# A list scheduler that counts the SBUF port of VectorE and GpSimd as a resource

## The chip, the core and the metric

The kernel runs on one core of a Trainium2 chip. The core's engines work side by side, each through its own queue in order: TensorE (PE; PEld is its weight load), VectorE (DVE), ScalarE (ACT), GpSimd (POOL) and SyncE (SP), which issues the DMAs. The metric is device time of one launch in microseconds (us); lower is better. Where one engine needs what another wrote, it waits on a semaphore.

## What is computed

Two transformer blocks of width 1024 on 512 tokens, in float32. The first has a state-space mixer (S5) and an attention that lets each query see the 128 keys with the highest index score; the second has retention, gated linear attention (GLA) and windowed attention with sinks, whose outputs are merged under gates, and a gated feed-forward layer.

```python
def reference(x, c, rel_bias, norm_g, w_ada, ...):
    x = first_block(x, c, rel_bias, norm_g, w_ada, ...)
    return second_block(x, norm_mix_pre_2, ...)

def first_block(x, c, ...):
    shift, scale, gate = split(silu(c) @ w_ada + b_ada)
    h = rms_norm(x, norm_g) * (1 + scale) + shift
    ssm_u, ssm_z, q, k, v, attn_z, q_idx, k_idx, w_idx = split(h @ w_in)
    y_ssm = s5_mixer(ssm_u, ...) * silu(ssm_z)
    y_attn = dsa_mixer(q, k, v, q_idx, k_idx, w_idx, ...) * silu(attn_z)
    return x + gate * (concat(y_ssm, y_attn) @ w_out)

def second_block(x, ...):
    (rq, rk, rv, rg, gq, gk, gv, gg, ga, sq, sk, sv, gate_logits) = split(rmsnorm(x) @ w_in)
    branches = stack(retention(rq, rk, rv), gla(gq, gk, gv, ga), swa_sinks(sq, sk, sv))
    x = x + rmsnorm(sum(sigmoid(gate_logits) * (branches @ w_branch)) @ w_out)
    h = rmsnorm(x)
    return x + rmsnorm((silu(h @ w_gate) * (h @ w_up)) @ w_down)
```

## The kernel before

A float32 product is computed from two parts of each operand: a rounded part (fp32r) and the rest. `wunit` loads a piece of a weight matrix into a tile `wr` by DMA, `copy` rounds it into `wh`, and `sub` subtracts, `wl = wr - wh`; both are 128 x 1024 and there are three buffers of each (NWH). Three matmuls then add up hi x hi, hi x lo and lo x hi in a PSUM tile `pm`. The activations are split in the same way (`split`). `proj_a` and `proj_b` are the two loops of the projections, by tokens and by output columns.

The order of the instructions is not that of the program text. `body` runs once and only records: each call on an engine object (`Engine.__getattr__`, line 439 issues them all later, so every row of the profile says L439) becomes an `Op` with its engine, its duration by a cost formula (`Engine.duration`), and the operations that it depends on. `Recorder.schedule` then walks through a simulated time: an engine that is free takes, out of its heap of ready operations, the one with the lowest key (program order, less boosts and less the length of the chain behind it), unless a buffer is missing. At one time the engines are asked in the order PE, DVE, ACT, POOL, SP. `issue` plays the list to the real engines, and each queue runs its part in that order; only data dependencies become waits on the chip.

Some operations may run on two engines: `copy` on ACT or DVE, `two` (an elementwise operation on two tensors) on DVE or POOL when nothing of it lies in PSUM. `Recorder.either` keeps both in `op.alts`. The engine that is asked takes it unless `better(op, e)` finds that the other one would finish sooner, counting what is ready there with a lower key, with a bonus of 300 ns for the other where DVE asks (YIELD). At most 24 operations are passed over in one look at a heap (`held`). By the cost formulas a `two` of 512 columns takes 610 on DVE and 1296 on POOL.

In the first 440 us lie the first block's modulation and projections, the index scores (`index_scores`: scalar_tensor_tensor on DVE), the search for the top 128 keys (`top_keys`: MAX8 and MATCH_REPLACE8 in turns on DVE), the S5 maps and phasors (`tap_map`, `s5_phasors`: many `two`) and the attention heads (`dsa_head`). The rest is the second block, where long runs of matmuls prevail.

Of the kernel before, what the change touches and what calls it, by code (L numbers as in the profile page):

```python
# [40 lines left out]
AVLATE = True  # L41
GATEAT = 3
YIELD = {("DVE", "ACT"): 300.0, ("DVE", "POOL"): 300.0}
WLIMIT = 400
NBOOST = 300
XRAHEAD = 100
# [39 lines left out]


class Op:
    __slots__ = ("idx", "eng", "call", "dur", "preds", "succs", "tiles", "key", "npred", "ready", "start", "end", "ahead", "alts", "table")


class Recorder:
# [50 lines left out]
    def either(self, *calls):  # L143

        self.options = []
        for c in calls:
            c()
        options, self.options = self.options, None
        self.record(*options[0])
        self.ops[-1].alts = {o[0]: (o[1], o[4]) for o in options}  # L150

    def record(self, eng, call, writes, reads, dur):
        if self.options is not None:
            self.options.append((eng, call, writes, reads, dur))
            return
        op = Op()
        op.alts = None
        op.table = self.table
        self.table = None
        op.idx = len(self.ops)  # L160
        op.eng, op.call, op.dur = eng, call, dur
        op.key = op.idx - self.boost
        op.ahead = self.ahead
        preds, tiles = set(), set()
        for ap in reads:
            name, cells = self._cells(ap)
            if name is None:
                continue
            tiles.add(name)
            cm = self.cells.setdefault(name, {})  # L170
            for c in cells:
                w = cm.get(c)
                if w is None:
                    w = cm[c] = [None, []]
                if w[0] is not None:
                    preds.add(w[0])
                w[1].append(op.idx)
        for ap in writes:
            name, cells = self._cells(ap)
            if name is None:  # L180
                continue
            tiles.add(name)
            cm = self.cells.setdefault(name, {})
            for c in cells:
                w = cm.get(c)
                if w is None:
                    w = cm[c] = [None, []]
                if w[0] is not None:
                    preds.add(w[0])
                preds.update(w[1])  # L190
                w[0], w[1] = op.idx, []
        preds.update(self.after)
        preds.discard(op.idx)
        op.preds = preds
        op.tiles = [t for t in tiles if t in self.info]
        self.ops.append(op)


    def schedule(self):
# [9 lines left out]
        for t in first:  # L209
            tag, bufs, _ = self.info[t]  # L210
# [3 lines left out]
        for tag, (bufs, ts) in tags.items():  # L214
# [6 lines left out]
            f, l = slot[tag]["first"], slot[tag]["last"]  # L221
# [58 lines left out]
        ready = {e: [] for e in engines}  # L280
# [15 lines left out]
        for op in ops:  # L296
            if op.npred == 0:
                arrive(op)
        dma_free = 0.0
        order = []  # L300
        freed = []
        now = 0.0
        front = 0
        choosy = True
        table = None

        def better(op, e):

            mine = now + op.alts[e][1]
            for f, (_, dur) in op.alts.items():  # L310
                if f != e:
                    t = max(free[f], now) + dur
                    for k, i in ready[f]:
                        if k < op.key and not done[i]:
                            t += ops[i].alts[f][1] if ops[i].alts else ops[i].dur
                    if t < mine + YIELD.get((e, f), 0.0):
                        return True
            return False

        while len(order) < n:  # L320
            if not events and choosy:
                choosy = False
                push(now, None)
            if not events:
                stuck = {e: [(ops[i].key, i) for _, i in ready[e]][:5] for e in engines}
                raise ValueError(f"no instruction can go on: {stuck}")
            now, _, what = heapq.heappop(events)
            if what is not None:
                for t in what:
                    left[t] -= 1  # L330
                    if left[t] == 0:
                        tag, bufs, _ = self.info[t]
                        if bufs:
                            s = slot[tag]
                            s["live"] -= 1
                            s["state"][s["pos"][t]] = 2
                            while s["lo"] < len(s["state"]) and s["state"][s["lo"]] == 2:
                                s["lo"] += 1
            if events and events[0][0] <= now:
                continue  # L340
            while front < n and done[front]:
                front += 1
            for e in engines:
                w = waiting[e]
                while w and w[0][0] <= now:
                    _, k, i = heapq.heappop(w)
                    heapq.heappush(ready[e], (k, i))
                while free[e] <= now and ready[e]:
                    held, got = [], None
                    while ready[e]:  # L350
                        k, i = heapq.heappop(ready[e])
                        op = ops[i]
                        if done[i]:
                            continue
                        if i > len(order) + op.ahead or (op.alts and choosy and better(op, e)):
                            held.append((k, i))
                            if len(held) >= 24:
                                break
                            continue
                        need = [t for t in op.tiles if self.info[t][1] and slot[self.info[t][0]]["state"][slot[self.info[t][0]]["pos"][t]] == 0]  # L360
                        if all(may_take(t, i, front) for t in need):
                            got = op
                            break
                        held.append((k, i))
                        if len(held) >= 24:
                            break
                    for h in held:
                        heapq.heappush(ready[e], h)
                    if got is None:
                        break  # L370
                    op = got
                    for t in need:
                        s = slot[self.info[t][0]]
                        s["live"] += 1
                        s["state"][s["pos"][t]] = 1
                    op.start = now
                    choosy = True
                    if op.alts:
                        op.eng = e
                        op.call, op.dur = op.alts[e]  # L380
                    if e == "SP":
                        free[e] = now + 450.0
                        dma_free = max(dma_free, now) + op.dur
                        op.end = max(dma_free, now + op.dur) + 2000.0
                    else:
                        load = 0.0
                        if e == "ACT" and op.table and op.table != table:
                            table, load = op.table, 1283.0
                        free[e] = now + load + op.dur
                        op.end = free[e]  # L390
                    push(free[e], None)
                    push(op.end + 150.0, tuple(op.tiles))
                    done[op.idx] = True
                    order.append(op)
                    for j in op.succs:
                        o2 = ops[j]
                        lat = self.LAT.get((op.eng, o2.eng), 197.0)
                        o2.ready = max(o2.ready, op.end + lat)
                        o2.npred -= 1
                        if o2.npred == 0:  # L400
                            arrive(o2)
# [4 lines left out]
def elems(ap):  # L406
    n = 1
    for _, c in ap.ap[1:]:
        n *= c
    return n  # L410


class Engine:
# [5 lines left out]
    def __getattr__(self, name):  # L419
        fn = getattr(self.real, name)  # L420

        def call(*args, **kw):
# [3 lines left out]
            writes = []  # L426
            reads = list(aps)
# [8 lines left out]
                self.rec.ahead = LOADAHEAD  # L436
            if self.eng == "ACT":
                self.rec.table = TABLES.get(args[2] if len(args) > 2 else kw.get("func"))
            self.rec.record(self.eng, lambda: fn(*args, **kw), writes, reads, self.duration(name, writes, reads, kw))  # L439
            if name == "memset":  # L440
                self.rec.ahead = 10 ** 9

        return call

    def duration(self, name, writes, reads, kw):
        out = writes[0]
# [1460 lines left out]
```

## Time and profile before

| | us |
|---|---|
| median of 3 runs | 1582.29 (1580.92 to 1583.3) |
| the profiled execution | 1583.61 |
| its span, first to last instruction | 1581.8 |
| PE busy, of the span | 1475.5 (93%) |
| DVE busy | 1040.0 (66%) |
| POOL busy | 377.6 (24%) |

The span is what the profile's rows are counted in, from the first instruction to the last; the profiled execution's own time has some 1.8 us around it. An engine's busy time is the time in which an instruction of it was under way, so an instruction that is under way and stands still counts as busy. The granted TensorE clock was 0.979 of full speed as a mean over the span.

### The profile page before, as it was taken

The numbers are of one execution on the slowest core, as the hardware profiler recorded it, in microseconds if no ns is written. First come the engines' busy times: TensorE is split into PE (matmuls) and PEld (weight loads), VectorE is DVE, ScalarE is ACT, GpSimd is POOL, SyncE is SP. The second block draws the span as 40 slices with busy tenths as digits, with TensorE's granted clock in tenths as the row PEclk, the third lists the DMA queues.
The fourth block names the chain that finished last, engine by engine and source line by source line (L and its number), as shares of the span: only waits on it lengthen the run. The fifth ranks groups of instructions, "written<-read, shape, count | busy, mean of one in ns | idle before, by whom it ended". The sixth has DMA issues, their size and how long they took to land.

```text
span 1581.8 us, 19335 instructions
## 1 busy us (share of the span) xinstructions
PE 1475.5 (93%) x7092; PEld 1210.0 (76%) x7092; DVE 1040.0 (66%) x2130; ACT 416.0 (26%) x905; POOL 377.6 (24%) x439
## 2 busy tenths in 40 slices
PE   6895988688999999989999999999999999999997
PEld 5674766577788887878887777778888888888886
DVE  5999995798874696696444777874478434443444
ACT  4351324344321132252011534431114111111010
POOL 2788741441200123020001221232120111110000
PEclk9997999899999999999999999999999999999999
DMA  8614232255613222213323223213343323333232
GB/s 235 203 40 156 82 79 51 67 149 180 213 49 127 62 78 83 81 35 99 106 81 120 94 67 105 69 54 106 118 151 118 106 88 99 107 96 104 81 133 107
DMA packets 169455, 165.26 MB, mean 104 GB/s; under 512 B 36992, under 2 KB 136200, under 8 KB 169232
## 3 DMA queue, kind: packets, MB, share of 16 engines
q1 hardware_dynamic: 169360, 164.02, 33.1%
q8 instruction: 56, 0.92, 0.2%
q14 instruction: 39, 0.32, 0.1%
HBM read 150.64 MB, written 10.47 MB: 102 GB/s over the span
## 4 chain that ended last, share of the span: by engine, by line
PE 65%; DVE 13%; DMA 2%; issue 2%; ACT 1%; POOL 1%; SPq 0%; DVEq 0%; ACTq 0%; POOLq 0%
PE pm L439 65%; DVE t L439 9%; DVE s L439 2%; DVE wl L439 1%; ACT t L439 1%; DMA wr<-w_in 1%; DMA wr<-w_ada 1%; POOL t L439 1%; DVE wh L439 1%; DVE c L439 0%; DMA t<-t 0%; SPq L439 0%; DMA t<-gla_w_alpha 0%; ACT L439 0%; ACT s L439 0%
## 5 line engine op out<-in xcount | busy, mean ns | idle before, releaser
L439 PE MATMUL pm<-c,wh 128*128 128x512 f32 (+1 forms) x1952 | 568.9, 388 | 4.5 <-DVE wh L439 2.5
L439 PEld LDWEIGHTS pm<-c,wh 128*128 128x128 f32 x1952 | 359.1, 189 | 75.5 <-DVE wh L439 3.4
L439 POOL TENSOR_TENSOR t<-t,t 128x512 f32<-128x512 f32 (+11 forms) x282 | 261.7, 941 | 627.7 <-ACT t L439 421.2
L439 DVE CAST wh<-wr 128x1024 fp32r<-128x1024 f32 x160 | 113.9, 712 | 356.4 <-PE pm L439 344.2
L439 PE MATMUL pm<-c,wl 128*128 128x512 f32 (+1 forms) x976 | 325.5, 387 | 0.6 <-DVE wl L439 0.5
L439 ACT ACTIVATE t<-pm 128x512 f32<-128x512 f32 (+8 forms) x315 | 150.1, 502 | 510.9 <-PE pm L439 488.0
L439 PE MATMUL pm<-t,t 128*128 128x256 f32 (+4 forms) x1232 | 242.3, 324 | 30.9 <-DVE t L439 18.2
L439 DVE TENSOR_TENSOR wl<-wr,wh 128x1024 fp32r<-128x1024 f32 (+2 forms) x195 | 244.1, 1255 | 24.3 <-PE pm L439 9.3
L439 PEld LDWEIGHTS pm<-t,t 128*128 128x128 f32 (+1 forms) x1232 | 193.7, 191 | 62.8 <-issue 14.2
L439 PEld LDWEIGHTS pm<-c,wl 128*128 128x128 f32 x976 | 183.1, 189 | 36.8 <-DVE wl L439 1.4
L439 PE MATMUL pm<-wh,c 128*128 128x512 f32 (+1 forms) x576 | 177.6, 391 | 4.0 <-DVE wh L439 2.5
L439 PE MATMUL pm<-c,t 128*128 128x128 f32 (+4 forms) x638 | 123.7, 307 | 30.9 <-DVE t L439 14.7
L439 PE MATMUL pm<-wh,t 128*128 128x512 f32 x480 | 142.2, 390 | 0.3 <-POOL t L439 0.3
L439 ACT ACTIVATE t<-t 128x512 fp32r<-128x512 f32 (+6 forms) x140 | 79.0, 581 | 229.2 <-DVE t L439 168.3
L439 PE MATMUL pm<-t,wh 128*128 128x512 f32 x416 | 137.2, 391 | 0.0
L439 PEld LDWEIGHTS pm<-c,t 128*128 128x128 f32 (+3 forms) x638 | 82.8, 152 | 64.2 <-issue 16.2
L439 PEld LDWEIGHTS pm<-wh,c 128*128 128x128 f32 x576 | 108.3, 192 | 26.9 <-DVE wh L439 3.2
L439 POOL TENSOR_TENSOR wl<-wr,wh 128x1024 fp32r<-128x1024 f32 (+1 forms) x17 | 42.7, 2513 | 320.6 <-DVE wh L439 200.6
L439 PE MATMUL pm<-wl,c 128*128 128x512 f32 (+1 forms) x288 | 104.6, 394 | 15.0 <-DVE wl L439 15.0
L439 ACT ACTIVATE wh<-wr 128x1024 fp32r<-128x1024 f32 (+2 forms) x52 | 52.9, 1019 | 203.9 <-PE pm L439 149.6
L439 PEld LDWEIGHTS pm<-wh,t 128*128 128x128 f32 x480 | 90.0, 188 | 20.0 <-POOL t L439 0.7
L439 DVE TENSOR_TENSOR t<-pm,t 64x256 f32<-64x256 f32 (+8 forms) x157 | 85.2, 557 | 24.8 <-ACT t L439 17.8
(113 smaller groups left out, 1346.4 us busy)
## 6 DMA issues: line engine op xcount, KB each, us to landing
wr<-w_in SPq DMA_DIRECT2D x48, 1024.0 KB, 5.0
wr<-w_branch SPq DMA_DIRECT2D x12, 1024.0 KB, 5.2
wr<-ffn_w_gate SPq DMA_DIRECT2D x11, 1024.0 KB, 5.2
wr<-ffn_w_up SPq DMA_DIRECT2D x11, 1024.0 KB, 5.2
wr<-ffn_w_down SPq DMA_DIRECT2D x10, 1024.0 KB, 5.0
wa<-w_ada SPq DMA_DIRECT2D x32, 256.0 KB, 4.3
wr<-w_out SPq DMA_DIRECT2D x8, 1024.0 KB, 4.9
wr<-w_in SPq DMA_DIRECT2D x12, 512.0 KB, 3.8
```

The source lines that it names most:

```text
L439: self.rec.record(self.eng, lambda: fn(*args, **kw), writes, reads, self.duration(name, writes, reads, kw))
```

## The change

Each recorded operation gets a flag `port`. `Engine.port` sets it: for POOL on all but `memset`; for DVE on operations with two or more SBUF inputs of more than one element per partition, and on `tensor_copy` and `tensor_scalar` (without `accum_out`) from SBUF to SBUF. The schedule keeps one time `port` until which the port is taken. An operation with the flag is passed over while that time lies ahead, and one that is taken sets it to its own end less HANDOVER, 60 ns on DVE and 150 ns on POOL; at that time the engines are asked again. The functions that choose between engines, the keys and the durations stay as they are, and `better` does not read the port.

```diff
--- before.py
+++ after.py
@@ -41,6 +41,7 @@
 AVLATE = True
 GATEAT = 3
 YIELD = {("DVE", "ACT"): 300.0, ("DVE", "POOL"): 300.0}
+HANDOVER = {"DVE": 60.0, "POOL": 150.0}
 WLIMIT = 400
 NBOOST = 300
 XRAHEAD = 100
@@ -86,7 +87,7 @@
 
 
 class Op:
-    __slots__ = ("idx", "eng", "call", "dur", "preds", "succs", "tiles", "key", "npred", "ready", "start", "end", "ahead", "alts", "table")
+    __slots__ = ("idx", "eng", "call", "dur", "preds", "succs", "tiles", "key", "npred", "ready", "start", "end", "ahead", "alts", "table", "port")
 
 
 class Recorder:
@@ -147,18 +148,18 @@
             c()
         options, self.options = self.options, None
         self.record(*options[0])
-        self.ops[-1].alts = {o[0]: (o[1], o[4]) for o in options}
-
-    def record(self, eng, call, writes, reads, dur):
+        self.ops[-1].alts = {o[0]: (o[1], o[4], o[5]) for o in options}
+
+    def record(self, eng, call, writes, reads, dur, port=False):
         if self.options is not None:
-            self.options.append((eng, call, writes, reads, dur))
+            self.options.append((eng, call, writes, reads, dur, port))
             return
         op = Op()
         op.alts = None
         op.table = self.table
         self.table = None
         op.idx = len(self.ops)
-        op.eng, op.call, op.dur = eng, call, dur
+        op.eng, op.call, op.dur, op.port = eng, call, dur, port
         op.key = op.idx - self.boost
         op.ahead = self.ahead
         preds, tiles = set(), set()
@@ -297,6 +298,7 @@
             if op.npred == 0:
                 arrive(op)
         dma_free = 0.0
+        port = 0.0
         order = []
         freed = []
         now = 0.0
@@ -307,7 +309,7 @@
         def better(op, e):
 
             mine = now + op.alts[e][1]
-            for f, (_, dur) in op.alts.items():
+            for f, (_, dur, _) in op.alts.items():
                 if f != e:
                     t = max(free[f], now) + dur
                     for k, i in ready[f]:
@@ -352,6 +354,11 @@
                         op = ops[i]
                         if done[i]:
                             continue
+                        if port > now and (op.alts[e][2] if op.alts else op.port):
+                            held.append((k, i))
+                            if len(held) >= 24:
+                                break
+                            continue
                         if i > len(order) + op.ahead or (op.alts and choosy and better(op, e)):
                             held.append((k, i))
                             if len(held) >= 24:
@@ -377,7 +384,10 @@
                     choosy = True
                     if op.alts:
                         op.eng = e
-                        op.call, op.dur = op.alts[e]
+                        op.call, op.dur, op.port = op.alts[e]
+                    if op.port:
+                        port = now + max(0.0, op.dur - HANDOVER[e])
+                        push(port, None)
                     if e == "SP":
                         free[e] = now + 450.0
                         dma_free = max(dma_free, now) + op.dur
@@ -436,11 +446,22 @@
                 self.rec.ahead = LOADAHEAD
             if self.eng == "ACT":
                 self.rec.table = TABLES.get(args[2] if len(args) > 2 else kw.get("func"))
-            self.rec.record(self.eng, lambda: fn(*args, **kw), writes, reads, self.duration(name, writes, reads, kw))
+            self.rec.record(self.eng, lambda: fn(*args, **kw), writes, reads, self.duration(name, writes, reads, kw),
+                            self.port(name, writes, reads, kw))
             if name == "memset":
                 self.rec.ahead = 10 ** 9
 
         return call
+
+    def port(self, name, writes, reads, kw):
+
+        if self.eng == "POOL":
+            return name != "memset"
+        if self.eng != "DVE":
+            return False
+        big = [r for r in reads if elems(r) > 1 and not self.in_psum(r)]
+        copies = name in ("tensor_copy", "tensor_scalar") and "accum_out" not in kw
+        return len(big) > 1 or (len(big) == 1 and copies and not self.in_psum(writes[0]))
 
     def duration(self, name, writes, reads, kw):
         out = writes[0]
```

## Rows read from the trace of the kernel before

**Rows 1.** the page: busy us by engine; POOL in 40 slices of 39.5 us.

```profile
PE 1475.5 (93%) x7092; PEld 1210.0 (76%) x7092; DVE 1040.0 (66%) x2130; ACT 416.0 (26%) x905; POOL 377.6 (24%) x439
...
POOL 2788741441200123020001221232120111110000
```

**Rows 2.** windows: stretch, length, busy us (xinstructions) by engine, granted clock, DMA share, GB/s.

```profile
0.00:40.00 40.00, 27.24 (x99) 20.44 (x100) 23.85 (x110) 16.02 (x35) 7.94 (x23) 0.91 0.89 234
40.00:240.00 200.00, 165.60 (x752) 128.37 (x750) 194.37 (x490) 65.96 (x136) 144.08 (x208) 0.94 0.37 111
240.00:440.00 200.00, 169.95 (x947) 141.18 (x948) 156.04 (x296) 81.62 (x189) 64.27 (x90) 0.93 0.43 131
440.00:1560.00 1120.00, 1099.18 (x5239) 909.19 (x5238) 652.71 (x1196) 249.67 (x538) 161.30 (x118) 1.00 0.29 94
1560.00:1581.80 21.80, 13.48 (x60) 10.84 (x58) 13.07 (x43) 2.75 (x8) 0.00 (x0) 0.90 0.25 96
```

**Rows 3.** waits, 240:440: us in total, times, longest.

```profile
PE pm L439 <- DVE t L439: 20.7, 11, 8.3
```

**Rows 4.** timeline, 100 to 160 us: start, us, engine, line, operation, count [idle before].

```profile
103.07 0.18 DVE L439 TENSOR_TENSOR t<-t 128x32 f32<-128x32 f32 x1
111.37 8.98 POOL L439 TENSOR_TENSOR t<-t,t 128x512 f32<-128x512 f32 x7
115.45 1.10 DVE L439 TENSOR_TENSOR t<-t 128x32 f32<-128x32 f32 x1
...
119.07 31.34 POOL L439 TENSOR_TENSOR t<-t,t 128x512 f32<-128x512 f32 x23
...
132.46 0.79 PE L439 MATMUL pm<-wl,c 128*128 128x512 f32 x1 [14.45 <-DVE wl L439]
```

**Rows 5.** groups by shape, DVE, 40:240: count, busy us, mean ns, idle before.

```profile
L439 DVE TENSOR_TENSOR wl<-wr,wh 128x1024 fp32r<-128x1024 f32 x14 | 19.8, 1417 | 0.1
L439 DVE TENSOR_TENSOR t<-t 128x32 f32<-128x32 f32 x47 | 15.5, 348 | 0.5 <-POOL t L439 0.2
L439 DVE MAX8 s<-t 128x8 f32<-128x512 f32 x16 | 10.8, 675 | 0.0
L439 DVE SCALAR_TENSOR_TENSOR t<-t,c,t 128x256 f32<-128x256 f32 x7 | 8.6, 1225 | 0.0
L439 DVE SCALAR_TENSOR_TENSOR t<-t,c,t 128x384 f32<-128x384 f32 x7 | 8.1, 1160 | 0.0
L439 DVE MATCH_REPLACE8 t<-s,t 128x512 f32<-128x512 f32 x15 | 10.0, 670 | 0.0
L439 DVE SCALAR_TENSOR_TENSOR t<-wa,c,t 128x256 f32<-128x256 f32 x16 | 7.8, 487 | 0.1
```

**Rows 6.** groups by shape, DVE, 440:520.

```profile
L439 DVE TENSOR_TENSOR wl<-wr,wh 128x1024 fp32r<-128x1024 f32 x11 | 13.3, 1222 | 2.0 <-ACT wh L439 1.8
L439 DVE TENSOR_TENSOR t<-t,t 128x512 f32<-128x512 f32 x2 | 1.4, 688 | 0.0
```

**Rows 7.** groups by shape, DVE, 240:440.

```profile
L439 DVE TENSOR_TENSOR t<-t,t 128x512 f32<-128x512 f32 x28 | 28.6, 1029 | 2.4 <-DMA t<-t 1.2 <-ACT t L439 0.8
L439 DVE TENSOR_TENSOR t<-wr,t 128x512 fp32r<-128x512 f32 x6 | 5.9, 1039 | 0.0
```

**Rows 8.** groups by shape, DVE, 440:1560.

```profile
L439 DVE TENSOR_TENSOR wl<-wr,wh 128x1024 fp32r<-128x1024 f32 x164 | 206.2, 1260 | 24.0 <-PE pm L439 9.3 <-ACT wh L439 5.7 <-issue 2.7
L439 DVE TENSOR_TENSOR t<-t,s 128x512 f32<-128x512 f32 x16 | 18.0, 1156 | 0.1
```

**Rows 9.** windows of instructions on pm alone: PE, PEld, DVE, ACT, clock, DMA.

```profile
40.00:240.00 200.00, 165.60 (x752) 128.37 (x750) 14.58 (x27) 46.64 (x107) 0.94 0.37 111
240.00:440.00 200.00, 169.95 (x947) 141.18 (x948) 52.14 (x103) 29.95 (x68) 0.93 0.43 131
```

**Rows 10.** groups by shape, POOL, 40:240.

```profile
L439 POOL TENSOR_TENSOR t<-t,t 128x512 f32<-128x512 f32 x48 | 63.6, 1348 | 0.1
```

**Rows 11.** groups by shape, POOL, 440:1560.

```profile
L439 POOL TENSOR_TENSOR wl<-wr,wh 128x1024 fp32r<-128x1024 f32 x9 | 23.9, 2651 | 207.5 <-DVE wh L439 111.7 <-PE pm L439 69.4 <-ACT wh L439 24.2
```

## The prediction

> **What bounds the kernel now.** I read the page's busy line first. TensorE (PE) is busy 1475.5 of 1581.8 us [rows 1], so PE is the bound as a whole and only its 106.3 us of idle time can come back, plus what a lowered clock costs. The windows then say where that idle time lies [rows 2]. In stretch A (40 to 240 us) PE is idle 200 - 165.60 = 34.4 us, in B (240 to 440 us) 30.0, in the long stretch C (440 to 1560 us) 1120 - 1099.18 = 20.8, at the start 12.8 and in the last 22 us 8.3. The reader is to see the DVE column beside it: VectorE (DVE) is busy 194.37 of 200 us in A, 156.04 in B, but 652.71 of 1120 in C. So A is bound by DVE, B partly, C by PE. The waits of PE agree: in B 20.7 us of them end with DVE tiles t [rows 3], and the longest of all, in A, ends with a DVE tile wl (below).
>
> Next I ask whether DVE in A works or waits. The timeline shows it [rows 4]. One and the same kind of DVE operation, 128x32 with its inputs in SBUF, takes 0.18 us at 103 us and 1.10 us at 115 us. GpSimd (POOL) runs 7 operations of 128x512 without a pause from 111.37 us on, and 23 more from 119.07 on, in 31.34 us. PE's 14.45 us wait, which ends at 132.46, falls in this time: the weight part wl that it needs stands in DVE's queue behind the stretched operations. So what counts as DVE busy holds waiting inside the instructions, and it is there only when POOL works.
>
> By shape it is as clear [rows 5]. In A the two-input SBUF operations are long: 1417 ns for a 128x1024 subtraction, 1225 ns for a scalar_tensor_tensor of 128x256. The 128x256 form whose input is a wa tile takes 487 ns. MAX8, with one input, takes 675 ns for 512 columns under the same POOL load. Where POOL does next to nothing (440 to 520 us, slices 12 and 13 of POOL's line in [rows 1]) the subtraction takes 1222 ns and a two-input 128x512 operation 688 ns [rows 6].
>
> **What the change does, part by part.** It alters only the plan that is made before the program is issued: which engine gets an operation that two could do, and the order on each engine. It adds no instruction, no DMA and no wait on the chip; the same arithmetic is issued. SP's queue is not a port user, and its DMAs move only as far as their producers or buffers move. So every gain or loss is a matter of order and of who does what.
>
> First, the wait in DVE that could be filled. In A, from [rows 5] against [rows 6] or against the shorter rows: wl 14 x (1417 - 1222) = 2.7 us; 128x32 47 x (348 - 180) = 7.9 us, with the 0.18 us of [rows 4]; 128x256 7 x (1225 - 487) = 5.2 us; 128x384 7 x (1160 - 590) = 4.0 us, where 590 is an estimate, halfway between 487 (256 columns) and 688 (512). Sum 19.8 us. In B the two largest groups [rows 7]: 28 x (1029 - 688) = 9.5 and 6 x (1039 - 688) = 2.1, sum 11.6 us. In C [rows 8]: 16 x (1156 - 688) = 7.5 and 164 x (1260 - 1222) = 6.2, sum 13.7 us.
>
> Second, how much of it returns. A wait is gained only when the planner has a DVE operation at hand that it does not count as a port user. Those are the ones with a PSUM input, 14.58 us in A and 52.14 in B [rows 9], and MAX8: 10.8 us for 512 columns [rows 5], and with the 384 and 256 widths in proportion (an estimate) 10.8 x 1152 / 512 = 24 us. That is 39 of 194 us in A, a fifth, and 52 of 156 in B, a third. Bounds of the share returned are 0 (those operations already run beside POOL, or are not ready) and 1 (every wait filled). I take a quarter in A and a third in B: A 5 us, B 4 us. In C PE is the bound and three weight buffers cover most DVE delays; PE's 20.8 us of idle time there is the ceiling. I take 2 us of 13.7; it costs up to 13.7 us if the cover fails.
>
> Third, what moves away from POOL. A 128x512 operation holds POOL 1348 ns in A, 48 times [rows 10]; DVE does it in 688 [rows 6]. With the port taken, POOL gets fewer of them and DVE more, and each that moves frees the port for 1348 - 688 = 0.66 us but costs DVE 0.69. While DVE waits behind POOL this is nearly a trade; I put 2 us gained on it, between 0 and 48 x 0.66 / 2 = 16 us (half of them moved). The casts that ScalarE may take as well are no help: the rule that picks between two engines does not look at the port, so ScalarE leaves a cast to a DVE that is free but barred. I count 0 there; ScalarE is busy only 65.96 of 200 us in A [rows 2] and would cover it.
>
> Start and tail: POOL is busy 7.94 us and 0 us there [rows 2], so 0. Sum: -5 - 4 - 2 - 2 = -13 us. The profiled execution took 1583.6 us (span 1581.8); it lies 1.3 us above the median of 1582.3. So 1583.6 - 13 = 1570.6, against the median 1569.3. I say 1570.
>
> A rule of the Trainium skill speaks against one detail. The trace shows MATCH_REPLACE8 at 670 ns for 512 columns, beside MAX8 at 675 and not stretched [rows 5]; the change marks it as a port user, since it reads the values and the eight maxima, and bars it while POOL works. "SBUF — State Buffer", section "Who interferes with whom", says that a DVE instruction with at most one SBUF input outside the two-port modes does not meet GpSimd at all; the row agrees that nothing is stretched. Were it unmarked, its 15 x 3 widths would add some 22 us of filler, and A's share would be a third: 7 us instead of 5.
>
> **Rivals.** (1) The port is full anyway. In A, DVE's 194.37 less 39 us of unmarked work is 155 us, and POOL has 144.08 [rows 2]: 299 us of port users in 200 us. If a single holder at a time is the truth, A lasts as long as its holders do, and order changes nothing; B and C lose their gain to the same. Against it: part of the 299 us is waiting, counted twice (19.8 us at least). It gives 0 in A, -2 in B, 0 else: about 1581. The Trainium skill, "SBUF — State Buffer", section "Who interferes with whom", says just this, an exclusive lock that is held for the whole instruction; by that rule A would keep its length unless operations leave POOL, about 1581 us again, and the 1.10 us of the 128x32 row agree with a lock.
>
> (2) Nothing happens because the plan is not followed. No semaphore ties the two engines to their turns, so the turns hold only as long as the plan's clock is right. The 14.45 us that PE waits in A [rows 4] are a sign that plan and chip differ. It gives 1583 plus or minus 3.
>
> (3) Slower: POOL wins the handover. In the plan the port comes free 60 ns before a DVE operation ends, while DVE itself is still taken; an idle POOL with something ready takes it then, every time, and holds it for a whole operation: 1348 ns in A [rows 10], 2651 ns for a wl in C [rows 11]. Meanwhile DVE is given less urgent work, and if that outlasts POOL's end, POOL takes the port again. Weights for PE (cast and wl, on DVE) come late. Place: A and B, and in C wherever POOL has a run. It decides when the extra turns on PE's path outnumber the gain: 13 / 1.35, some 10 turns. With 17 of them, 10 more than pay for 9 us: 1583 - 13 + 17 x 1.35 = 1593. For it: 118 POOL instructions in C, where little is to be gained. Against it: on the chip the two take turns already [rows 4], so most of these waits are in the old time too.
>
> (4) All the blocked time of A and B returns and half of what POOL gives up: 1583.6 - 31.4 - 8 = 1544.
>
> **How the numbers follow.** Forecast (1558 to 1579): 0.50. Rivals (1) and (2): 0.16 together, within 0.2% (3.2 us, about what a measurement of this kernel can tell from no change) for the most part; (3): 0.26; (4): 0.08. Faster: 0.50 + 0.08 + 0.02 from (1) = 0.60; same 0.15 (0.14 and 0.01 of the third); slower 0.25. The range leaves out half of (4) and the upper third of (3): 1549 to 1592.
>
> **What would show it.** Right: in 40 to 240 us the 128x32 and 128x256 two-input rows on DVE fall towards 180 and 487 ns, POOL has fewer 128x512 operations, and the wait of PE for wl shrinks from 14.45 us. C's PE idle time stays near 21 us. Rival (1): the stretched rows shrink, yet PE's idle time in A stays 34 us. Rival (2): those rows keep their means. Rival (3): PE's idle time in C grows, its waits ending on DVE wh and wl. The forecast is wrong if the first 440 us do not get shorter, whatever DVE's rows do.

## The result and the profile after

The changed kernel takes 1557.82 us (1556.93 to 1561.91, 4 runs) beside 1581.61 for the one before: a ratio of 0.9854, 95% interval 0.9833 to 0.9874, 23.8 us less. I had forecast 13 us less. The profiled execution took 1556.93 us, its span is 1555.1 us, 26.7 less than before.

The page of after: busy time by engine, POOL's 40 slices, and the shares of the chain that ended last.

```profile
PE 1465.6 (94%) x7092; PEld 1210.6 (78%) x7092; DVE 1000.6 (64%) x2098; ACT 434.1 (28%) x911; POOL 373.2 (24%) x465
...
POOL 1148694662200123020000232332210111110000
...
PE 74%; DVE 5%; DMA 1%; ACT 1%; issue 1%; POOL 1%; SPq 0%; DVEq 0%; ACTq 0%; POOLq 0%
```

The same chain line of before:

```profile
PE 65%; DVE 13%; DMA 2%; issue 2%; ACT 1%; POOL 1%; SPq 0%; DVEq 0%; ACTq 0%; POOLq 0%
```

PE is busy 9.9 us less than in [rows 1] and idle 1555.1 - 1465.6 = 89.5 us against 106.3. DVE is busy 39.4 us less. The reader is to see the chain: DVE's share of it fell from 13% to 5%. What the page does not show is where. The windows of after for stretches A and B are (columns as in [rows 2]):

```profile
40.00:240.00 200.00, 171.19 (x819) 138.68 (x819) 183.11 (x481) 70.63 (x124) 122.17 (x234) 0.93 0.36 110
240.00:440.00 200.00, 166.36 (x902) 135.62 (x902) 164.99 (x318) 80.70 (x193) 83.54 (x95) 0.93 0.45 133
```

In A PE is idle 28.8 us (34.4 in [rows 2]), in B 33.6 (30.0). So A and B together gained 2 us by this measure, where I had looked for 9. The stretches hold other work than before, though, so I cut both runs where the work itself cuts them. SP writes the result of the first block to the tensor scr_xd in 8 DMAs, and that of the second block's mixers in 8 more. Timeline of SP in after, merged rows that end with the 8th and with the 16th of these writes:

```profile
425.94 15.13 SPq L449 DMA_DIRECT2D scr_xd<-t  x5
...
1174.24 13.44 SPq L449 DMA_DIRECT2D scr_xd<-t  x6
```

The 8th starts at 440.7 us and the 16th at 1187.4; in before they start at 447.8 and 1214.1. Windows by these stages, the first block, the mixers, the feed-forward layer, before:

```profile
0.00:447.80 447.80, 370.10 (x1832) 295.84 (x1833) 381.40 (x912) 166.20 (x364) 216.29 (x321) 0.94 0.44 130
447.80:1214.10 766.30, 747.14 (x3609) 615.36 (x3608) 504.18 (x1008) 208.51 (x471) 129.50 (x97) 1.00 0.29 92
1214.10:1581.80 367.70, 358.22 (x1656) 298.83 (x1654) 154.46 (x212) 41.31 (x72) 31.80 (x21) 0.99 0.31 101
```

and after:

```profile
0.00:440.70 440.70, 365.55 (x1833) 295.97 (x1834) 373.80 (x904) 169.01 (x352) 210.09 (x341) 0.93 0.45 132
440.70:1187.40 746.70, 741.77 (x3608) 615.78 (x3606) 472.38 (x985) 223.84 (x489) 131.23 (x103) 1.00 0.30 94
1187.40:1555.10 367.70, 358.24 (x1656) 298.87 (x1653) 154.45 (x212) 41.30 (x72) 31.87 (x21) 0.99 0.30 101
```

Of the 26.7 us, 7.1 were gained in the first block, 19.6 in the mixers (766.3 to 746.7), and 0.0 in the feed-forward layer. PE's idle time in the mixers went from 766.30 - 747.14 = 19.2 us to 4.9. The other 5.4 us left its busy time, though the number of matmuls is the same within one. They are pauses too. In the profile a matmul of 512 columns lasts some 0.39 us where the next one starts 0.23 us after it, so the first part of each pause counts as busy. Counted by starts (each interval to the next matmul, less the median interval for its shape, where it is over 30 ns longer), pauses make up 45.0 us of the mixers before and 26.2 after, some 19 us less.

### The profile page after: what moved, and what is told of

The parts are those of the page before. It is cut to its first block, busy times and chain, and to the rows that moved or that the text cites. A ratio compares the mean times of both kernels' runs of the same rounds, so it can differ in the third digit from the quotient of the medians.

```text
span 1555.1 us, 19327 instructions
## 1 busy us (share of the span) xinstructions
PE 1465.6 (94%) x7092; PEld 1210.6 (78%) x7092; DVE 1000.6 (64%) x2098; ACT 434.1 (28%) x911; POOL 373.2 (24%) x465
## 4 chain that ended last, share of the span: by engine, by line
PE 74%; DVE 5%; DMA 1%; ACT 1%; issue 1%; POOL 1%; SPq 0%; DVEq 0%; ACTq 0%; POOLq 0%
PE pm L449 74%; DVE t L449 4%; ACT t L449 1%; DMA t<-t 1%; DVE s L449 1%; POOL t L449 0%; SPq L449 0%; DMA wr<-w_in 0%; DMA wr<-w_out 0%; DVE wl L449 0%; DVE c L449 0%; POOL wl L449 0%; DMA t<-scr_kd 0%; ACT wh L449 0%; DVE wh L449 0%
## 5 line engine op out<-in xcount | busy, mean ns | idle before, releaser
L449 POOL TENSOR_TENSOR t<-t,t 128x512 f32<-128x512 f32 (+11 forms) x267 | 239.0, 910 | 576.2 <-ACT t L449 408.5
L449 PE MATMUL pm<-c,wl 128*128 128x512 f32 (+1 forms) x976 | 327.1, 388 | 11.8 <-DVE wl L449 10.3
L449 DVE CAST wh<-wr 128x1024 fp32r<-128x1024 f32 (+1 forms) x141 | 97.7, 693 | 355.1 <-PE pm L449 347.1
L449 DVE TENSOR_TENSOR wl<-wr,wh 128x1024 fp32r<-128x1024 f32 (+2 forms) x186 | 231.4, 1247 | 33.3 <-ACT wh L449 14.7
L449 PEld LDWEIGHTS pm<-t,t 128*128 128x128 f32 (+1 forms) x1232 | 192.1, 192 | 48.7 <-DVE t L449 11.5
L449 PE MATMUL pm<-wh,c 128*128 128x512 f32 (+1 forms) x576 | 173.1, 385 | 0.0
L449 PE MATMUL pm<-t,wh 128*128 128x512 f32 x416 | 143.4, 396 | 4.7 <-ACT t L449 3.8
L449 ACT ACTIVATE t<-t 128x512 fp32r<-128x512 f32 (+6 forms) x149 | 84.4, 577 | 223.7 <-DVE t L449 163.8
L449 POOL TENSOR_TENSOR wl<-wr,wh 128x1024 fp32r<-128x1024 f32 (+2 forms) x26 | 60.6, 2333 | 351.3 <-DVE wh L449 236.3
L449 PE MATMUL pm<-c,t 128*128 128x128 f32 (+4 forms) x638 | 114.5, 299 | 18.7 <-DVE t L449 8.1
L449 ACT ACTIVATE wh<-wr 128x1024 fp32r<-128x1024 f32 (+2 forms) x71 | 73.3, 1034 | 189.7 <-PE pm L449 153.5
L449 DVE TENSOR_TENSOR t<-t,t 128x512 f32<-128x512 f32 (+11 forms) x157 | 103.4, 673 | 5.4 <-ACT t L449 2.1
```

## Experiments

All numbers of stages are from the profiled executions, cut at the 8th and 16th write to scr_xd in the same way. "Bars DVE" says whether the plan makes DVE pass over a port user while the port is taken.

| kernel | bars DVE | time, us | first block | mixers | rest |
|---|---|---|---|---|---|
| before | no | 1581.6 | 447.8 | 766.3 | 367.7 |
| b_jit1 | no | 1579.2 | 446.5 | 763.3 | 370.0 |
| b_jit2 | no | 1567.9 | 432.4 | 765.6 | 368.1 |
| pool_yields | no | 1568.3 | 431.2 | 767.6 | 367.7 |
| after | yes | 1557.8 | 440.7 | 746.7 | 367.7 |
| a_jit1 | yes | 1572.8 | 454.8 | 747.0 | 369.9 |
| a_jit2 | yes | 1579.9 | 469.6 | 742.8 | 367.9 |
| dve_yields | yes | 1570.0 | 452.6 | 747.5 | 367.8 |
| full_hold | yes | 1569.8 | 457.9 | 741.3 | 367.9 |
| mr_free | yes | 1546.5 | 429.2 | 748.5 | 367.8 |
| mr_jit1 | yes | 1557.8 | 438.8 | 746.9 | 371.5 |
| mr_jit2 | yes | 1580.8 | 468.4 | 743.1 | 367.8 |
| dve_blocks | counts the wait | 1570.1 | 454.5 | 746.1 | 367.7 |
| second_only | second block | 1563.8 | 447.4 | 745.8 | 367.9 |

**Is it the port, or the luck of another plan?** A list schedule turns a small change into a wholly different order, so I shook the plan of both kernels with the same small numbers and changed nothing else.

```diff
             op.key -= TAIL * tail[op.idx] / 1000.0
+            op.key += 4.0 * (op.idx * ODD % 4294967296) / 4294967296
```

ODD is 2901351343 in the first pair and 3148266925 in the second.

> The kernel before, with a fixed pseudo-random 0 to 4 added to each key (a key is a place in program order), so that the plan is another one of the same kind and still knows no port. If the port is the cause of the gain: within 8 us of 1582. If the gain is the luck of one reshuffled plan among many: the four jittered plans of both kinds scatter over some 30 us and overlap, and this one may as well come out at 1560.

> The same as the first jitter of the kernel before, with other random numbers. Port: within 8 us of 1582. Luck: anywhere from 1555 to 1595.

> The changed kernel with the jitter in its keys, the port in the plan. Port: within 8 us of 1558, below both jittered plans of the kernel before. Luck: anywhere from 1555 to 1595, with no order between the two kinds.

> The same with other random numbers. Port: within 8 us of 1558. Luck: anywhere from 1555 to 1595.

The jittered plans of before took 1579.2 and 1567.9 us (ratios 0.9984 and 0.9921), those of after 1572.8 and 1579.9 (0.9945 and 0.9993). They overlap: one reshuffle of the old plan alone gains nearly 14 us, and one of the new plan gives nearly all its gain away. By the total, "port" as I had written it is refuted and "luck" looks right. The stages tell the two apart. In the first block the six plans scatter from 432 to 470 us without order. In the mixers they do not scatter: 763 to 766 without the port in the plan, 743 to 747 with it. So the gain in the mixers belongs to the change, and the 7.1 us of the first block can't be told from luck.

The scatter has its place in the trace. Wait of PE in a_jit2, from 240 us to the end of its first block:

```profile
PE pm L450 <- DVE t L450: 44.5, 10, 14.8
```

PE stood for up to 14.8 us at a time, in places where a chain through DVE came late; the same line in [rows 3] has 20.7 us with 8.3 as the longest. By shape and place, the 14.8 us stand before the matmuls of the first block's gate (`load_gate`), whose DVE operations had themselves waited 5.1 us for a DMA of `w_ada`, and the next two, 11.8 and 9.1, before the output matmuls of the S5 mixer (`s5_batch`). So blocked DVE operations are not all that makes the first block scatter.

**Which half of the rule?** One kernel bars POOL alone, one DVE alone.

```diff
-if port > now and (op.alts[e][2] if op.alts else op.port):
+if e == "POOL" and port > now and (...):      # pool_yields
+if e == "DVE" and port > now and (...):       # dve_yields
```

> Half of the rule: an operation on POOL is passed over while the port is taken, one on DVE is not. If the gain comes from keeping POOL from taking the port before DVE: about all of it, 1558 to 1565. If it comes from DVE doing unmarked work while POOL holds the port (the term of my sum): little of it, 1575 to 1582.

> The other half: DVE is passed over while the port is taken, POOL is not. If the gain is DVE's filled waits: most of it, 1558 to 1568. If it is POOL's restraint: little, 1575 to 1590, since POOL then takes even more of the port.

They took 1568.3 us (0.9917) and 1570.0 (0.9937). Each lies between its two expected ranges, which says nothing by itself. By stages it is plain: the mixers take 767.6 us when POOL alone is barred, as before, and 747.5 when DVE alone is. The window of pool_yields over its mixers has PE idle 20.0 us, like before:

```profile
431.20:1198.80 767.60, 747.56 (x3610) 614.69 (x3608) 503.64 (x1010) 213.13 (x476) 120.51 (x90) 1.00 0.29 91
```

That of dve_yields has 5.3:

```profile
452.60:1200.10 747.50, 742.17 (x3608) 613.99 (x3607) 482.79 (x998) 215.30 (x478) 129.37 (x103) 1.00 0.30 94
```

So the whole gain of the mixers comes from what the plan knows of DVE. POOL's restraint, alone, changes nothing there. The 1568.3 us of pool_yields lies in its first block, 431.2.

**Does DVE fill its waits, or does the plan only know the time?** This was the step that the sum rested on. Here DVE takes its most urgent operation though the port is taken, and the plan adds the wait to it; POOL is barred as in the changed kernel.

```diff
-if port > now and (...):
+if port > now and e != "DVE" and (...):
...
+wait = max(0.0, port - now) if op.port else 0.0
 if op.port:
-    port = now + max(0.0, op.dur - HANDOVER[e])
+    port = now + wait + max(0.0, op.dur - HANDOVER[e])
...
-load = 0.0
+load = wait
```

> The plan gives DVE its most urgent operation even when the port is taken, and counts the wait as part of it, as the chip does; POOL is passed over as in the changed kernel. So the plan's clock knows the port, but DVE does no other work meanwhile. What the runs so far show: from the end of the first block to the end, plans that bar DVE take 1082 to 1089 us and plans that do not 1105 to 1107. If that gain is filled waiting time on DVE (my term): about 1105 here. If it is the truer clock, by which PE's queue is ordered: 1083 to 1090. The whole time adds the first block, 434 to 474 us in the runs so far, and so says less.

The 1082 to 1107 us in this expectation, and in that of second_only below, were counted from a mark 3 to 5 us later to 22 to 24 us before the end; they stand for 1109 to 1135 us of mixers and rest in the table. It took 1570.08 us (0.9936), and its mixers and rest 1113.8: the range of the truer clock. The mixers take 746.1 us, within 1 us of the changed kernel, although DVE fills nothing. Window over its mixers and PE's waits in it:

```profile
454.50:1200.60 746.10, 739.79 (x3610) 614.35 (x3608) 490.42 (x981) 227.90 (x502) 122.47 (x94) 1.00 0.30 94
```

```profile
PE pm L450 <- ACT t L450: 2.3, 4, 1.1
PE pm L450 <- POOL t L450: 1.7, 2, 1.1
PE pm L450 <- DVE s L450: 0.8, 1, 0.8
```

PE is idle 6.3 us, and DVE is busy 490.42 us, between 504.18 before and 472.38 after. One group shows best that DVE still stands at the port: the multiplication of windowed attention's probabilities by their reciprocal sums (t<-t,s), in the mixers. Before,

```profile
L439 DVE TENSOR_TENSOR t<-t,s 128x512 f32<-128x512 f32 x16 | 18.0, 1156 | 0.1
```

with dve_blocks,

```profile
L450 DVE TENSOR_TENSOR t<-t,s 128x512 f32<-128x512 f32 x12 | 13.8, 1166 | 0.1
```

and after,

```profile
L449 DVE TENSOR_TENSOR t<-t,s 128x512 f32<-128x512 f32 x11 | 10.2, 936 | 0.1
```

At 1166 ns it is as stretched as before, and yet PE hardly waits for it. Over wl, the weight casts and the 128x512 operations t<-t,s and t<-t,t (mean less the mean of 440 to 520 us in before: 1222, 693 and 688 ns), I estimate DVE's stretching in the mixers at 21 us before, 18 with dve_blocks and 12 after. So it is not DVE's waiting time that was won: dve_blocks won back some 2 us of it, and the mixers are 20 us shorter. PE's queue is in order, and the plan writes that order by the times at which it believes tiles to be there. Before, it did not count the port, so matmuls stood in the queue ahead of others that were ready. The trace of before shows one such place, timeline of POOL, DVE and PE:

```profile
944.69 4.49 POOL L439 TENSOR_TENSOR t<-t,s 128x512 f32<-128x512 f32 x3
...
942.35 1.22 DVE L439 TENSOR_TENSOR wl<-wr,wh 128x1024 fp32r<-128x1024 f32 x1
...
943.87 1.40 DVE L439 CAST wh<-wr 128x1024 fp32r<-128x1024 f32 x1
945.20 1.52 DVE L439 TENSOR_TENSOR t<-t,s 128x512 f32<-128x512 f32 x1
946.64 2.06 DVE L439 TENSOR_TENSOR wl<-wr,wh 128x1024 fp32r<-128x1024 f32 x1
...
946.87 0.85 PE L439 MATMUL pm<-c,t 128*128 128x128 f32 x6 [1.37 <-DVE t L439]
947.47 0.36 PE L439 MATMUL pm<-t,t 128*128 128x256 f32 x1
947.67 0.40 PE L439 MATMUL pm<-c,wl 128*128 128x512 f32 x1
```

and a group of the same kernel, 440 to 520 us:

```profile
L439 DVE CAST wh<-wr 128x1024 fp32r<-128x1024 f32 x8 | 5.5, 693 | 18.3 <-PE pm L439 18.3
```

POOL multiplies three tiles in 4.49 us. Beside it a cast takes 1.40 us (693 ns where it is free) and the multiplication 1.52 (688 in [rows 6]): 1.54 us more than unhindered, and the plan knew nothing of it. PE, which was to transpose that tile next, stands for 1.37 us. Behind the transposes in its queue, at 947.67, is a weight matmul on a wl. The last wl before it was written by 943.57 us and the next is under way until 948.70, and nothing wrote the activations c that it reads from 941 to 948 us. So this matmul was ready all that time and stood in line. Waits of PE in the mixers of before:

```profile
PE pm L439 <- DVE t L439: 5.9, 10, 1.4
PE pm L439 <- DVE s L439: 5.4, 7, 1.2
PE pm L439 <- DVE wh L439: 2.5, 2, 2.1
PE pm L439 <- POOL t L439: 2.3, 2, 1.5
```

and after:

```profile
PE pm L449 <- DVE s L449: 1.8, 1, 1.8
PE pm L449 <- ACT t L449: 1.4, 3, 0.8
PE pm L449 <- DVE t L449: 0.7, 2, 0.5
```

I put the 5.9, 5.4, 2.5 and 2.3 us before down to this kind, though I followed only the one place above; what is left after are a few single waits. That the order of PE's queue is the means is argued from this; no run fixed that order alone. The plan's clock also moves operations between engines, and no run held these fixed. But no move goes with the gain. In the mixers ScalarE makes 34 weight casts in pool_yields (767.6 us), and only 31 in dve_yields (747.5) and 32 in full_hold (741.3). DVE has 1002 to 1010 instructions in the four plans without the gain, and 1032 in full_hold. POOL has 86 to 97 in those four, and 51 to 103 in the ten with it.

**Only in the second block.** The flag is set for operations recorded behind the first block's last projection, that is for the whole second block; the line stands ahead of its mixers.

```diff
+rec.shared = True          # ahead of merged = [None] * KT
...
-self.port(name, writes, reads, kw))
+self.rec.shared and self.port(name, writes, reads, kw))
```

> The flag is set only for operations recorded in the second block. If the rule's gain lies there alone and the first block only scatters: the first block as before, 450 to 455 us, the rest 1082 to 1090, in all 1560 to 1567. If the rule also shortens the first block by the 9 us of my terms A and B: the first block is 9 us longer than in the changed kernel, which has 445, and the total some 1566.

It took 1563.75 us (0.9892; 0.9864 to 0.9921). Its first block and mixers:

```profile
0.00:447.40 447.40, 368.49 (x1832) 294.87 (x1833) 381.81 (x912) 167.27 (x364) 216.13 (x321) 0.94 0.44 130
447.40:1193.20 745.80, 740.73 (x3609) 614.78 (x3608) 472.28 (x984) 223.92 (x489) 131.26 (x103) 1.00 0.30 94
```

The first block takes 447.4 us, as before (447.8), the mixers 745.8. That is the cleanest measure of the rule: 20.5 us in the mixers, by themselves. Mixers and rest are 1113.7 us, as expected for a gain that lies there alone.

**The handover.** HANDOVER is 0 on both engines, so the port comes free when the operation ends, and DVE asks first.

```diff
-HANDOVER = {"DVE": 60.0, "POOL": 150.0}
+HANDOVER = {"DVE": 0.0, "POOL": 0.0}
```

> HANDOVER set to 0 on both engines: the port is held to the operation's end, and DVE and POOL ask for it at the same instant, DVE first. If the early handover to POOL costs (my slower rival as a part of the result): faster than the changed kernel, 1548 to 1555. If it does not matter which of the two goes first: 1558 give or take 5.

1569.84 us (0.9926). The stages differ in sign from the total:

```profile
0.00:457.90 457.90, 370.28 (x1836) 299.10 (x1837) 374.05 (x1023) 164.26 (x354) 123.00 (x220) 0.90 0.43 127
457.90:1199.20 741.30, 738.34 (x3603) 613.69 (x3602) 486.74 (x1032) 221.06 (x492) 50.52 (x51) 1.00 0.30 95
```

The mixers are the shortest of all, 741.3 us, 1.5 us below the next; POOL is busy 50.52 us there instead of 131.23, so who wins the handover decides who gets the work. The first block of 457.9 us, inside its scatter, takes it back. That the early handover costs anything in the mixers is not shown: the other nine plans with the gain differ among themselves by 5.7 us (742.8 to 748.5). For the whole, neither expectation was met.

**MATCH_REPLACE8 unmarked,** alone and with the two jitters:

```diff
-if self.eng != "DVE":
+if self.eng != "DVE" or name == "match_replace":
     return False
```

> The changed kernel with MATCH_REPLACE8 not marked as a port user. My estimate of the detail: 2 us faster than the changed kernel, 1556. If the mark does nothing or the reshuffle of the plan outweighs it: within 8 us of 1558 on either side.

> The kernel with MATCH_REPLACE8 unmarked (1546) with the same jitter of keys as the first jittered plans. If the wrong mark costs time in the first block: first block near 434 to 445, total 1545 to 1558, below the jittered plans with the mark (1573 and 1580). If 1546 was a lucky plan: a first block anywhere from 434 to 474, total 1546 to 1586.

> The same with the second set of random numbers; its marked counterpart took 1580. Mark: 1545 to 1558. Luck: 1546 to 1586.

1546.46 us (0.9778; 0.9750 to 0.9807): it beats both kernels, and is the fastest here, faster than either expectation (1556, or 1550 to 1566). With the jitters it takes 1557.8, with a first block of 438.8 us as the mark's expectation has it, and 1580.8, which only luck's range holds. Against the marked kernel of the same jitter, the first block is shorter by 440.7 - 429.2 = 11.5, 454.8 - 438.8 = 16.0 and 469.6 - 468.4 = 1.2 us; the mixers, where there are no such operations, move by 1.8, 0.1 and 0.3. Three pairs of one sign speak for the mark costing time, but a first block scatters by 40 us, so this is not shown. 1546 itself is in part a lucky plan, as the same rule takes 1580.8 with the second jitter.

## Why the prediction was right and where it was not

The direction held, and the time lies in the range of 1549 to 1592, though 0.2 us below the 1558 to 1579 that had the forecast's 0.50. The size was about half, and the place was wrong. That the total came out is partly luck. The changed kernel and its two jittered plans average 1570.2 us, those of before 1576.2: 6 us apart, and with the second jitter the changed rule is the slower one by 12. By my own last sign the forecast's mechanism failed: beyond its scatter, the first block did not get shorter.

- **Term C, 2 us, was the mis-sized one: 19.6 us.** I bounded the gain by filled waits, took PE for the bound and trusted the weight buffers. But the ceiling stood in my own rows: 20.8 us of PE idle time in C [rows 2], and I did not ask what ended those waits. In the mixers 16.1 of 19.2 us of it ended with tiles of DVE or POOL. I had written that PE's idle time in C would stay near 21 us; it went to 1093.30 - 1087.21 = 6.1 (440 us to 21.8 us before the end), and to 4.9 in the mixers. The filling share had nothing to do with it: dve_blocks fills nothing and gains the same.
- **Terms A and B, 9 us, and 2 us for work leaving POOL.** The first block gave 7.1 us. Jittered plans put the first block anywhere from 432 to 470, so the agreement proves nothing. Plans with the full rule and the mark in the first block (after, a_jit1, a_jit2) average 455.0 us, those without (before, b_jit1, b_jit2) 442.2; if the rule does anything there, it is not a gain. What I said of the rows came partly true. DVE, groups by shape, 40 to 240 us, after:

```profile
L449 DVE TENSOR_TENSOR wl<-wr,wh 128x1024 fp32r<-128x1024 f32 x13 | 16.0, 1229 | 1.8 <-ACT wh L449 1.8
L449 DVE TENSOR_TENSOR t<-t 128x32 f32<-128x32 f32 x20 | 8.9, 464 | 0.1
L449 DVE SCALAR_TENSOR_TENSOR t<-t,c,t 128x384 f32<-128x384 f32 x7 | 4.2, 606 | 0.0
L449 DVE SCALAR_TENSOR_TENSOR t<-t,c,t 128x256 f32<-128x256 f32 x7 | 3.3, 474 | 0.0
```

  The 128x256 form fell from 1225 to 474 ns, 128x384 from 1160 to 606, wl from 1417 to 1229; the waits inside are nearly gone. The 128x32 form did not fall, 464 against 348, but 20 are left of 47, since POOL has most of them now. POOL, same stretch:

```profile
L449 POOL TENSOR_TENSOR t<-t,t 128x512 f32<-128x512 f32 x28 | 35.1, 1264 | 1.0 <-DVE t L449 0.7
L449 POOL TENSOR_TENSOR t<-t 128x32 f32<-128x32 f32 x80 | 22.4, 291 | 48.7 <-DVE t L449 46.0 <-DVE c L449 1.4
```

  The 128x512 operations went from 48 [rows 10] to 28, as said. PE's wait for wl in A is still there:

```profile
PE pm L449 <- DVE wl L449: 12.7, 2, 10.3
```

  Its longest is 10.3 us, against 14.45 [rows 4]. So the rule did what it says, DVE is blocked less, and the stage still ends when it did, give or take the plan.
- **ScalarE, counted at 0.** It took 19 more weight casts (52 to 71 in the whole kernel, 28 to 38 in the mixers). The rule that chooses engines does not look at the port, but it adds up what is ready on DVE with a lower key, and passed-over operations stay in that heap. That is how I read the code; no run tested it.
- **Rivals.** (1), the port is full: it fits the first block in so far as shorter DVE rows did not shorten it beyond the scatter, but no run shows that a full port is the reason; it is wrong for the mixers. (2), the plan is not followed: refuted in the mixers, where second_only changes nothing but the plan and gains 20.5 us; it is the other way round, the plan was not followed before. (3), POOL wins the handover: its sign, more idle time of PE in C, did not come; full_hold's mixers are 5.4 us shorter than those of after, which plans with the rule differ by anyway. Its price was worded the wrong way round: 10 turns use up the 13 us, and 7 more make the loss of 9. (4): the 1546 us of mr_free is near its price, but that kernel has another mark and in part a lucky plan, so it does not bear on it.
- **What I left out** was the luck of the plan. My range took in mechanisms only; jitter without any mechanism moves the old plan by 14 us and the new one by 22.

## What to carry to other kernels

When a planner's cost model is changed, shake the plan with meaningless jitter on both sides first: here totals overlapped, and only cutting the runs at stage marks separated a steady 20 us from a scatter of 40. A planner gains by knowing when things are late even where it can't make them earlier; the likely reason is that in-order queues are ordered by what it believes. So where the bound engine has idle time, read who ends each wait before calling it covered.

## What the runs showed of the hardware

VectorE's operations with two SBUF inputs stand still inside their busy time while GpSimd works: 128x32 took 1.10 us instead of 0.18 [rows 4], so the cost reaches operations of hardly any size. MAX8 and MATCH_REPLACE8 on 512 columns do not: between 119.07 and 150.4 us, where POOL ran without a pause [rows 4], six of each took 675 and 668 ns as means, and between 150.45 and 162.5, where POOL did nothing, three of each took 676 and 670. One wide input is not what decides, for the cast from SBUF to SBUF has one too and took 1.40 us beside POOL instead of 0.69. And the cost matters more as an error of time than as lost time: with the multiplication as stretched as before (1166 ns), the mixers were 20 us shorter.
